# Seven block products of a gated feed-forward: lower left weights loaded twice, products reordered, operand sums in other buffers

## The chip, the cores and the metric

The kernel runs on one core of a Trainium2 chip. The metric is the device time of one execution in microseconds (us); less is better.

## What is computed

Two transformer blocks follow each other on 512 tokens of width 1024, all in float32. The first has a gated feed-forward network, a mixer (short convolution and attention), and a second gated feed-forward; the second block has its own mixer and feed-forward. The change touches the second feed-forward of the first block alone (`ffn2` in the inputs):

```python
def swiglu(x, w_gu, w_down):
    g, u = jnp.split(x @ w_gu, 2, axis=-1)
    return (jax.nn.silu(g) * u) @ w_down
...
        u = modulate(rmsnorm(h, norm3_g[l]), mod[:, 2, 0], mod[:, 2, 1])
        h = h + FFN_RES_WEIGHT * mod[:, 2, 2][:, None, :] * swiglu(u, ffn2_w_gu[l], ffn2_w_down[l])
```

The inner width is 2816, so `w_gu` is 1024 x 5632 and `w_down` 2816 x 1024.

## The kernel before

**How a float32 product is made.** Each operand is cut into a high part (`hi`, rounded by ScalarE on the copy) and a low part (`lo`, the rest, by VectorE); TensorE then adds three products, hi x hi, hi x lo and lo x hi. Line 131 makes `whi`, line 132 `wlo` of a weight tile; both kinds have four buffers. This is called a split below.

**How the stage is tiled.** The 2816 inner features are 22 blocks of 128, taken two at a time: 11 pairs. The first pair (`eight_pair`, line 652) multiplies in the plain way, lines 162 to 164. The other ten (`seven_pair`, line 670) take the gate block and the up block of the weights together as a 2 x 2 block matrix (rows: upper and lower half of the 1024 inputs; columns: gate and up), the activations as a 2 x 2 block matrix too (columns: upper and lower half of the tokens), and make the product with seven block products in place of eight, lines 536, 541 and 543. One block product is 24 matmuls of 256 columns, so a pair has 168.

**What the seven products need.** `load` (line 555) fetches the four weight blocks of a pair, each 128 x 1024 float32 (512 KB): w11 and w12 are the gate's upper and lower half of rows, w21 and w22 the up block's. w11 and w21 lie in tiles of the tag `ra` (four buffers), w12 and w22 together in one `raw` tile, of which there are two in the whole kernel; the weights of the down projection come through these two as well. `run` (line 571) needs four sums of weight blocks. They are made by DMAs that add into their target (line 578), issued by GpSimd; they work in place, so a sum that is written over a block has to wait until the split of that block has read it. On the other side the products need four sums of activation blocks, `usum` (lines 512 to 518), made once by VectorE in `operand` (line 508), split into `uth` and `utl`, and held for the whole stage. The tiles of `usum` take the four `ra` buffers too.

**The order in `run` before.** Products are named p1, p2, q7, q5, q6, q3, q4, in this order. p1, p2 and q3 multiply plain activations; q4 to q7 multiply sums of them.

```python
            p1 = split_w(w11)
            add(w11, w21)
            ...
            q7 = split_w(w11)
            add(w21, w22)
            add(w11, w22)
            ...
            q6 = split_w(w11)
            add(w11, w12)
            ...
            q3 = split_w(w11)
```

The results stand in four PSUM banks (`ca`, `cb`, `cc`, `cd`); ScalarE copies three of them out (line 582), VectorE combines them (lines 607 to 617), `upper` applies the gate function and `lower` multiplies and splits the result for the down projection.

**What sets the order of the work.** The framework orders the instructions of each engine when the kernel is built, by program order and by its own idea of when each can start; on the chip each engine then works through its list in that order, and an instruction that waits holds up all behind it on its engine. Loads are issued by SyncE's queue (SP), the adding DMAs by GpSimd's (POOL).

**Around it.** The pairs come in groups: pairs 2 to 4 of the stage, then a down projection of six features, again three pairs and six features, three and six, then one pair and the last four features (`bounds`, line 688). The down projection (lines 162 to 164 with `m_hi`, `m_lo`) is 128 x 512 matmuls.

Of the kernel before, what the change touches and what calls it, by code (L numbers as in the profile page):

```python
# [8 lines left out]
F32 = mybir.dt.float32  # L9
# [4 lines left out]
P = 128  # L14
D = 1024
# [10 lines left out]
def kernel(  # L26
# [7 lines left out]
    nc = tc.nc  # L34
# [13 lines left out]
    def z_bank(shape=(P, S)):  # L48
        return ps.tile(list(shape), F32, tag="z", name="z_ps")
# [32 lines left out]
    with tc.tile_pool(name="stage", bufs=1) as stage:  # L82
# [41 lines left out]
        def split_w(src, hi=None, lo=None):  # L124
            if hi is None:
                shape = [P, src.shape[1], src.shape[2]]
                hi, lo = (
                    wp.tile([P, 8 * P], F32R, tag=tag, name=tag, bufs=4)[
                        :, 0:shape[1] * shape[2]].rearrange("p (k n) -> p k n", n=shape[2])
                    for tag in ("whi", "wlo"))  # L130
            nc.scalar.activation(out=hi, in_=src, func=AF.Copy)  # L131
            nc.vector.tensor_tensor(out=lo, in0=src, in1=hi.bitcast(F32), op=ALU.subtract)  # L132
            return hi, lo
# [184 lines left out]
        class Modulated:  # L318
# [13 lines left out]
            def operand(self):  # L332
                u = new_u()
                for pb, cols in self.pieces:
                    modulate(self.sub, u, pb, cols)
                return u
# [163 lines left out]
    class Seven:  # L500
# [4 lines left out]
            self.pool = pool  # L505
            self.sums = []

        def operand(self, u, full):

            self.u = u  # L510
            for k in range(HK):
                t = self.pool.tile([P, 4, 256], F32, tag="ra", name="usum", bufs=4)
                b11, b12 = full[k][:, H1], full[k][:, H2]
                b21, b22 = full[k + HK][:, H1], full[k + HK][:, H2]
                nc.vector.tensor_sub(out=t[:, 0], in0=b11, in1=b12)
                nc.vector.tensor_sub(out=t[:, 2], in0=b12, in1=b22)
                nc.vector.tensor_sub(out=t[:, 1], in0=t[:, 2], in1=b11)
                nc.vector.tensor_add(out=t[:, 3], in0=t[:, 1], in1=b21)
                hi, lo = (self.pool.tile([P, 4, 256], F32R, tag=tag, name=tag, bufs=HK)
                          for tag in ("uth", "utl"))  # L520
                nc.scalar.activation(out=hi, in_=t, func=AF.Copy)
                nc.vector.tensor_tensor(out=lo, in0=t, in1=hi.bitcast(F32), op=ALU.subtract)
                self.sums.append((hi, lo))
# [31 lines left out]
        def load(self, a1, a2):  # L555
            def block(out, src):
                nc.sync.dma_start(out=out, in_=src.rearrange("(k p) n -> p k n", p=P))

            half = D // 2
            w11, w21 = (self.pool.tile([P, HK, 256], F32, tag="ra", name="w_sum", bufs=4)  # L560
                        for _ in range(2))
            raw = raw_tile()
            w12, w22 = (raw[:, i * 1024:(i + 1) * 1024].rearrange("p (k n) -> p k n", n=256)
                        for i in range(2))
            block(w11, a1[0:half])
            block(w21, a2[0:half])
            block(w12, a1[half:D])
            block(w22, a2[half:D])
            return w11, w12, w21, w22

        def run(self, weights, upper, lower):

            w11, w12, w21, w22 = weights

            def add(to, of):
                nc.gpsimd.dma_start(out=to, in_=of, accum_op=ALU.add)

            def copy(acc):  # L580
                v = self.ev()
                nc.scalar.activation(out=v, in_=acc, func=AF.Copy)
                return v

            p1 = split_w(w11)
            add(w11, w21)
            ca = z_bank()
            self.times(ca, p1, self.plain(0, H1), True)
            v1 = copy(ca)
            p2 = split_w(w12)  # L590
            self.times(ca, p2, self.plain(HK, H1), False)
            upper(ca, 0)
            q7 = split_w(w11)
            add(w21, w22)
            add(w11, w22)
            cd = z_bank()
            self.times(cd, q7, self.diff(2), True)
            v7 = copy(cd)
            q5 = split_w(w21)
            cc = z_bank()  # L600
            self.times(cc, q5, self.diff(0), True)
            v5 = copy(cc)
            q6 = split_w(w11)
            add(w11, w12)
            cb = z_bank()
            self.times(cb, q6, self.diff(1), True)
            nc.vector.tensor_add(out=v1, in0=v1, in1=cb)
            nc.vector.tensor_add(out=v5, in0=v5, in1=v1)
            nc.vector.tensor_sub(out=v7, in0=v7, in1=v5)
            q3 = split_w(w11)  # L610
            self.times(cc, q3, self.plain(HK, H2), False)
            nc.vector.tensor_add(out=v5, in0=cc, in1=v1)
            upper(v5, 1)
            lower(v7, 1)
            q4 = split_w(w22)
            self.times(cd, q4, self.diff(3), False)
            nc.vector.tensor_sub(out=v1, in0=cd, in1=v1)
            lower(v1, 0)

# [13 lines left out]
    def ffn_seven(nxt, w_gu, w_down, sub, on_final):  # L633
        with tc.tile_pool(name=f"ffn{sub}", bufs=4) as fp:
# [9 lines left out]
            def split_m(m, hi, lo):  # L644
                nc.scalar.activation(out=hi, in_=m, func=AF.Copy)
                nc.vector.tensor_tensor(out=lo, in0=m, in1=hi.bitcast(F32), op=ALU.subtract)

            def m_pair():
                return tuple(fp.tile([P, 2, S], F32R, tag=tag, name=name)
                             for tag, name in (("mh", "m_hi"), ("ml", "m_lo")))  # L650

            def eight_pair(f0):
                pair = m_pair()
                for r in range(2):
                    f = f0 + r
                    wg, wu = by_feature(load_pair(w_gu[:, f * P:(f + 1) * P],
                                                  w_gu[:, FF + f * P:FF + (f + 1) * P], KT, P))
                    for cols in (ALL,) if r else HALVES:
                        n = cols.stop - cols.start
                        pg = mm_bank()[:, 0:n]  # L660
                        proj(pg, wg, u, cols=cols)
                        pu = mm_bank()[:, 0:n]
                        proj(pu, wu, u, cols=cols)
                        sg = seven.ev()[:, 0:n]
                        nc.scalar.activation(out=sg, in_=pg, func=AF.Silu)
                        nc.vector.tensor_mul(out=sg, in0=sg, in1=pu)
                        split_m(sg, *(t[:, r, cols] for t in pair))
                return pair

            def seven_pair(f0):  # L670
# [15 lines left out]
                return pair  # L686

            bounds = ((0, 6), (6, 12), (12, 18), (18, 22))
            pairs = [eight_pair(0)]
            seven.operand(u, full)  # L690
            for f0, f1 in bounds:
                last = f1 == NF
                for f in range(f0 + 2, min(f1 + 2, NF), 2):
# [755 lines left out]
```

## Time and profile before

| what | value |
|---|---|
| three runs | 2166.06 us (median), 2164.12 to 2168.78 |
| the profiled execution | 2169.28 us |
| its span, first to last instruction | 2167.5 us |
| granted TensorE clock, mean of the span | 0.986 |
| TensorE (PE) busy | 2099.1 us, 97% |
| VectorE (DVE) busy | 1242.4 us, 57% |
| ScalarE (ACT) busy | 882.7 us, 41% |
| GpSimd (POOL) busy | 127.7 us, 6% |

PE is the matrix engine, PEld its weight load, which runs beside it. Times within the trace count from the first instruction. The seven-product stage lies between 810 us and 1171 us. In a timeline row the columns are start, duration, engine, line, operation, written tile, read tiles, shapes, number, and in brackets the idle time of that engine before the instruction and what ended it. A "q" behind an engine's name marks its queue. A row of busy time by stretch has the stretch, its length, then for PE, PEld, DVE, ACT and POOL the busy time and the number of instructions, then the granted clock, the share of time that the DMA engines were busy, and GB/s.

### The profile page before, as it was taken

The page shows a single profiled execution, that of the slowest core. Times are in us where ns is not written, and L with a number is a line of the kernel's source. Part 1 is how long each engine was busy: PE and PEld are TensorE (multiplying, and loading weights), DVE is VectorE, ACT ScalarE, POOL GpSimd, SP SyncE. Part 2 cuts the span into 40 slices and gives each one's busy share as a digit, 9 for nine tenths or more (in the row PEclk, how much of TensorE's full clock was granted, in tenths as well). Part 3 has the DMA queues.
Part 4 walks back from the last instruction along what each step waited for, and adds up shares of the span by engine and source line. Part 5 has one row for each costly group of instructions (what it writes and reads, how often), then busy time and mean ns, then how long its engine had stood idle before and what let it go on. Part 6 is the DMA issues. An engine that isn't in the chain of part 4 may idle for free.

```text
span 2167.5 us, 26690 instructions
## 1 busy us (share of the span) xinstructions
PE 2099.1 (97%) x10522; PEld 1737.5 (80%) x10522; DVE 1242.4 (57%) x2104; ACT 882.7 (41%) x1372; POOL 127.7 (6%) x196
## 2 busy tenths in 40 slices
PE   7999999999999997899989999998999999999998
PEld 5778888888878887888888877766888888888888
DVE  3775645557543474545456477754554566474665
ACT  4322222367643353333334454554233344242444
POOL 1000000000000001010100011111400000000000
PEclk9999999999999999999999999999999999999999
DMA  9766644331223336565544242221423333333332
GB/s 344 225 218 174 195 142 124 107 98 59 59 79 98 97 100 139 151 135 155 134 129 110 78 122 78 78 73 59 136 78 97 98 98 98 97 97 98 88 117 79
DMA packets 287569, 256.81 MB, mean 118 GB/s; under 512 B 7525, under 2 KB 269354, under 8 KB 287188
## 3 DMA queue, kind: packets, MB, share of 16 engines
q1 hardware_dynamic: 278336, 223.96, 33.9%
q0 software_dynamic: 8416, 30.06, 6.4%
q8 instruction: 83, 1.36, 0.3%
q10 hardware_dynamic: 692, 1.09, 0.1%
q14 instruction: 42, 0.34, 0.1%
HBM read 229.89 MB, written 4.23 MB: 108 GB/s over the span
## 4 chain that ended last, share of the span: by engine, by line
PE 47%; ACT 1%; issue 1%; DVE 1%; DMA 0%; POOL 0%; POOLq 0%; ACTq 0%; DVEq 0%
PE mm_ps L162 12%; PE mm_ps L164 12%; PE mm_ps L163 12%; PE mm_ps L174 2%; PE mm_ps L175 2%; PE mm_ps L176 2%; PE po_ps L1133 2%; PE z_ps L1126 1%; PE z_ps L1087 1%; PE z_ps L1089 1%; PE z_ps L543 0%; PE z_ps L541 0%; PE z_ps L536 0%; PE z_ps L1248 0%; DMA w_sum<-w_raw 0%
## 5 line engine op out<-in xcount | busy, mean ns | idle before, releaser
L131 ACT ACTIVATE whi<-w_raw 128x1024 fp32r<-128x1024 f32 (+2 forms) x338 | 344.4, 1023 | 704.7 <-PE mm_ps L163 550.4
L162 PE MATMUL mm_ps<-uh,whi 128*128 128x512 f32 (+1 forms) x1360 | 529.4, 391 | 5.1 <-ACT uh L307 2.0
L163 PE MATMUL mm_ps<-ul,whi 128*128 128x512 f32 x1360 | 529.5, 390 | 0.0
L164 PE MATMUL mm_ps<-uh,wlo 128*128 128x512 f32 x1360 | 528.4, 389 | 0.0
L132 DVE TENSOR_TENSOR wlo<-w_raw,whi 128x1024 fp32r<-128x1024 f32 (+2 forms) x338 | 402.3, 1193 | 149.7 <-ACT whi L131 145.6
L162 PEld LDWEIGHTS mm_ps<-uh,whi 128*128 128x128 f32 x1360 | 255.8, 189 | 60.7 <-ACT uh L307 3.9
L164 PEld LDWEIGHTS mm_ps<-uh,wlo 128*128 128x128 f32 x1360 | 256.0, 188 | 52.1 <-issue 1.6
L163 PEld LDWEIGHTS mm_ps<-ul,whi 128*128 128x128 f32 x1360 | 256.1, 188 | 51.8 <-issue 0.8
L162 PE MATMUL mm_ps<-m_hi,whi 128*128 128x512 f32 (+1 forms) x560 | 211.6, 381 | 0.9 <-ACT whi L131 0.5
L163 PE MATMUL mm_ps<-m_lo,whi 128*128 128x512 f32 (+1 forms) x560 | 211.3, 377 | 0.0
L164 PE MATMUL mm_ps<-m_hi,wlo 128*128 128x512 f32 (+1 forms) x560 | 211.1, 378 | 0.0
L162 PEld LDWEIGHTS mm_ps<-m_hi,whi 128*128 128x128 f32 x560 | 105.4, 188 | 21.1 <-ACT whi L131 0.9
L163 PEld LDWEIGHTS mm_ps<-m_lo,whi 128*128 128x128 f32 x560 | 105.5, 188 | 20.2 <-issue 0.4
L164 PEld LDWEIGHTS mm_ps<-m_hi,wlo 128*128 128x128 f32 x560 | 105.3, 188 | 20.0
L132 DVE TENSOR_TENSOR wlo<-w_sum,whi 128x1024 fp32r<-128x1024 f32 x50 | 61.2, 1225 | 103.8 <-ACT whi L131 103.0
L536 PE MATMUL z_ps<-uth,whi 128*128 128x256 f32 x320 | 94.6, 296 | 18.7 <-ACT whi L131 18.6
L174 PE MATMUL mm_ps<-whi,uh 128*128 128x512 f32 (+1 forms) x288 | 100.7, 353 | 5.9 <-ACT zv L1190 2.9
L131 ACT ACTIVATE whi<-w_sum 128x1024 fp32r<-128x1024 f32 x50 | 52.9, 1058 | 126.4 <-DMA w_sum<-w_raw 69.5
L175 PE MATMUL mm_ps<-wlo,uh 128*128 128x512 f32 (+1 forms) x288 | 99.0, 345 | 0.0
L176 PE MATMUL mm_ps<-whi,ul 128*128 128x512 f32 (+1 forms) x288 | 97.8, 345 | 0.0
L543 PE MATMUL z_ps<-uth,wlo 128*128 128x256 f32 x320 | 93.7, 293 | 3.6 <-DVE wlo L132 3.6
L541 PE MATMUL z_ps<-utl,whi 128*128 128x256 f32 x320 | 92.8, 290 | 0.0
(355 smaller groups left out, 3261.4 us busy)
## 6 DMA issues: line engine op xcount, KB each, us to landing
w_raw<-in_ffn_w_gu_dram SPq DMA_DIRECT2D x68, 512.0 KB, 5.2
ada_w<-in_w_ada_dram SPq DMA_DIRECT2D x28, 1024.0 KB, 5.2
w_raw<-in_w_up_dram SPq DMA_DIRECT2D x44, 512.0 KB, 5.2
w_raw<-in_w_in_dram SPq DMA_DIRECT2D x20, 1024.0 KB, 5.2
w_sum<-w_raw POOLq DMA_DIRECT2D x30, 512.0 KB, 4.6
w_raw<-in_ffn_w_down_dram SPq DMA_DIRECT2D x16, 768.0 KB, 4.4
w_raw<-in_w_mix_in_dram SPq DMA_DIRECT2D x24, 512.0 KB, 5.3
w_sum<-in_ffn_w_gu_dram SPq DMA_DIRECT2D x20, 512.0 KB, 3.6
```

The costliest lines, as they stand in the source:

```text
L131: nc.scalar.activation(out=hi, in_=src, func=AF.Copy)
L132: nc.vector.tensor_tensor(out=lo, in0=src, in1=hi.bitcast(F32), op=ALU.subtract)
L162: nc.tensor.matmul(acc, lhsT=a, rhs=uhi[:, cols], start=k == 0, stop=False)
L163: nc.tensor.matmul(acc, lhsT=a, rhs=ulo[:, cols], start=False, stop=False)
L164: nc.tensor.matmul(acc, lhsT=b, rhs=uhi[:, cols], start=False, stop=k == n - 1)
L174: nc.tensor.matmul(acc, lhsT=a, rhs=wh, start=k == 0, stop=False)
L175: nc.tensor.matmul(acc, lhsT=a, rhs=wl, start=False, stop=False)
L176: nc.tensor.matmul(acc, lhsT=b, rhs=wh, start=False, stop=k == kt - 1)
L536: i = nc.tensor.matmul(a, lhsT=whi[:, k, rows], rhs=uhi, start=start and first is None, stop=False, skip_group_check=True)
L541: nc.tensor.matmul(a, lhsT=whi[:, k, rows], rhs=ulo, start=False, stop=False, skip_group_check=True)
L543: nc.tensor.matmul(a, lhsT=wlo[:, k, rows], rhs=uhi, start=False, stop=last, skip_group_check=True)
L1133: nc.tensor.matmul(po[64 * hd:64 * hd + 64, b * P:S], lhsT=vts[head // 4][:, b, c0:c0 + 64], rhs=pT, start=b == 0, stop=b == NB - 1, skip_ ...
```

## The change

`load` fetches w21 a second time, into a third tile `s1`; the tag `ra` has five buffers in place of four. In `run`, `s1` becomes w21 + w22, then takes w11, then w12, one after the other; `w21` itself takes w11. So w11, w12 and w22 stay as loaded, and the first two sums, `add(s1, w22)` and `add(w21, w11)`, write over nothing that a split reads before. The order of products becomes q5, q7, p1, q6, p2, q4, q3. The loads come in the order s1, w22, w11, w21, w12. `usum` takes its tiles from the tag `ml` (which the low parts of the results use later), and its work moves from behind the first pair to the place between the two halves of it, before the buffers for that pair's result are taken.

```diff
-        def operand(self, u, full):
+        def operand(self, u, full, tag):
             self.u = u
+            self.raw = [self.pool.tile([P, 4, 256], F32, tag=tag, name="usum")
+                        for _ in range(HK)]
+            self.full = full
+
+        def steps(self):
             for k in range(HK):
-                t = self.pool.tile([P, 4, 256], F32, tag="ra", name="usum", bufs=4)
...
-            w11, w21 = (self.pool.tile([P, HK, 256], F32, tag="ra", name="w_sum", bufs=4)
-                        for _ in range(2))
+            w11, w21, s1 = (self.pool.tile([P, HK, 256], F32, tag="ra", name="w_sum", bufs=5)
+                            for _ in range(3))
...
+            block(s1, a2[0:half])
+            block(w22, a2[half:D])
             block(w11, a1[0:half])
             block(w21, a2[0:half])
             block(w12, a1[half:D])
-            block(w22, a2[half:D])
...
+            add(s1, w22)
+            add(w21, w11)
+            q5 = split_w(s1)
+            add(s1, w11)
+            cc = z_bank()
+            self.times(cc, q5, self.diff(0), True)
+            v5 = copy(cc)
+            q7 = split_w(w21)
+            cd = z_bank()
+            self.times(cd, q7, self.diff(2), True)
+            v7 = copy(cd)
             p1 = split_w(w11)
-            add(w11, w21)
             ca = z_bank()
             self.times(ca, p1, self.plain(0, H1), True)
             v1 = copy(ca)
+            q6 = split_w(s1)
+            add(s1, w12)
+            cb = z_bank()
+            self.times(cb, q6, self.diff(1), True)
+            nc.vector.tensor_add(out=v1, in0=v1, in1=cb)
             p2 = split_w(w12)
             self.times(ca, p2, self.plain(HK, H1), False)
             upper(ca, 0)
-            q7 = split_w(w11)
-            add(w21, w22)
-            add(w11, w22)
-            cd = z_bank()
-            self.times(cd, q7, self.diff(2), True)
-            v7 = copy(cd)
-            q5 = split_w(w21)
-            cc = z_bank()
-            self.times(cc, q5, self.diff(0), True)
-            v5 = copy(cc)
-            q6 = split_w(w11)
-            add(w11, w12)
-            cb = z_bank()
-            self.times(cb, q6, self.diff(1), True)
-            nc.vector.tensor_add(out=v1, in0=v1, in1=cb)
             nc.vector.tensor_add(out=v5, in0=v5, in1=v1)
             nc.vector.tensor_sub(out=v7, in0=v7, in1=v5)
-            q3 = split_w(w11)
+            q4 = split_w(w22)
+            self.times(cd, q4, self.diff(3), False)
+            q3 = split_w(s1)
             self.times(cc, q3, self.plain(HK, H2), False)
             nc.vector.tensor_add(out=v5, in0=cc, in1=v1)
             upper(v5, 1)
             lower(v7, 1)
-            q4 = split_w(w22)
-            self.times(cd, q4, self.diff(3), False)
             nc.vector.tensor_sub(out=v1, in0=cd, in1=v1)
             lower(v1, 0)
...
             def eight_pair(f0):
-                pair = m_pair()
+                made = []
...
+                        made.append((sg, r, cols))
+                    if r == 0:
+                        seven.steps()
+                        pair = m_pair()
+                    for sg, r, cols in made:
                         split_m(sg, *(t[:, r, cols] for t in pair))
+                    made = []
...
+            seven.operand(u, full, "ml")
             pairs = [eight_pair(0)]
-            seven.operand(u, full)
```

## Rows read from the trace of the kernel before

**Rows 1.** The page: span, share and count of TensorE; its granted clock by slice.

```profile
PE 2099.1 (97%) x10522; PEld 1737.5 (80%) x10522; DVE 1242.4 (57%) x2104; ACT 882.7 (41%) x1372; POOL 127.7 (6%) x196
...
PEclk9999999999999999999999999999999999999999
```

**Rows 2.** Busy time by stretch: the four groups of seven-product pairs.

```profile
810.00:899.00 89.00, 72.42 (x512) 69.16 (x511) 41.54 (x49) 31.86 (x42) 10.59 (x12) 0.90 0.64 153
930.00:1008.00 78.00, 69.37 (x511) 67.42 (x511) 38.74 (x44) 30.95 (x40) 7.83 (x9) 0.91 0.63 151
1040.00:1118.00 78.00, 68.20 (x508) 65.87 (x508) 38.73 (x44) 30.73 (x40) 7.84 (x9) 0.93 0.58 138
1150.00:1171.00 21.00, 21.00 (x174) 20.82 (x173) 10.70 (x14) 8.72 (x13) 0.87 (x1) 1.00 0.41 98
```

**Rows 3.** The same view: the first pair, and a down projection.

```profile
782.00:810.00 28.00, 25.33 (x152) 21.79 (x153) 25.36 (x58) 22.93 (x44) 0.70 (x1) 1.00 0.28 87
...
1118.00:1150.00 32.00, 32.00 (x145) 26.52 (x144) 16.64 (x20) 8.73 (x11) 2.61 (x3) 1.00 0.43 109
```

**Rows 4.** Timeline of TensorE, two matmuls of a block product without a wait.

```profile
951.14 0.28 PE L541 MATMUL z_ps<-ul,whi 128*128 128x256 f32 x1
951.26 0.28 PE L543 MATMUL z_ps<-uh,wlo 128*128 128x256 f32 x1
```

**Rows 5.** Groups by line from 810 to 1171 us: TensorE's idle time, last columns.

```profile
L536 PE MATMUL z_ps<-uth,whi 128*128 128x256 f32 x320 | 94.6, 296 | 18.7 <-ACT whi L131 18.6
...
L543 PE MATMUL z_ps<-uth,wlo 128*128 128x256 f32 x320 | 93.7, 293 | 3.6 <-DVE wlo L132 3.6
L536 PE MATMUL z_ps<-uh,whi 128*128 128x256 f32 x240 | 74.1, 309 | 12.2 <-ACT whi L131 10.5 <-ACT ev L582 1.7
```

**Rows 6.** Timeline of ScalarE: the splits of the second seven-product pair, and the next.

```profile
832.32 1.04 ACT L131 ACTIVATE whi<-w_sum 128x1024 fp32r<-128x1024 f32 x1
...
845.00 1.06 ACT L131 ACTIVATE whi<-w_sum 128x1024 fp32r<-128x1024 f32 x1 [2.22 <-DMA w_sum<-w_sum]
...
852.54 1.06 ACT L131 ACTIVATE whi<-w_sum 128x1024 fp32r<-128x1024 f32 x1 [0.69 <-DMA w_sum<-w_raw]
...
860.25 1.06 ACT L131 ACTIVATE whi<-w_sum 128x1024 fp32r<-128x1024 f32 x1 [2.90 <-DMA w_sum<-w_raw]
...
862.16 1.04 ACT L131 ACTIVATE whi<-w_sum 128x1024 fp32r<-128x1024 f32 x1
```

**Rows 7.** Timeline of VectorE: the low part of one split.

```profile
846.08 1.22 DVE L132 TENSOR_TENSOR wlo<-w_sum,whi 128x1024 fp32r<-128x1024 f32 x1 [2.58 <-ACT whi L131]
```

**Rows 8.** Timeline of GpSimd: two sums of the same pair, issue only.

```profile
835.29 0.87 POOL L578 DMA_DIRECT2D w_sum<-w_sum  x1 [8.62 <-DVE wlo L132]
845.17 0.87 POOL L578 DMA_DIRECT2D w_sum<-w_raw  x1 [9.01 <-DMA w_sum<-w_sum]
```

**Rows 9.** Waits from 810 to 1171 us: us in total, times, longest.

```profile
POOL w_sum L578 <- DVE wlo L132: 244.8, 28, 36.8
```

**Rows 10.** DMA issues from 800 to 1171 us, last column median us to landing.

```profile
w_sum<-w_raw POOLq DMA_DIRECT2D x30, 512.0 KB, 4.6
w_sum<-in_ffn_w_gu_dram SPq DMA_DIRECT2D x20, 512.0 KB, 3.6
...
w_raw<-in_ffn_w_gu_dram SPq DMA_DIRECT2D x16, 512.0 KB, 5.2
w_sum<-w_sum POOLq DMA_DIRECT2D x10, 512.0 KB, 6.7
```

**Rows 11.** The sums of line 578 alone: from issue to landing.

```profile
DMA to landing us min/median/max: 4.5/4.7/9.6
```

**Rows 12.** Timelines of SyncE's queue and VectorE: first block loads, last activation sum.

```profile
804.16 28.95 SPq L557 DMA_DIRECT2D w_sum<-in_ffn_w_gu_dram  x6
...
806.94 1.22 DVE L522 TENSOR_TENSOR utl<-usum,uth 128x1024 fp32r<-128x1024 f32 x1
```

**Rows 13.** Timeline of TensorE: the first matmul of the seven-product stage.

```profile
810.18 0.28 PE L536 MATMUL z_ps<-uh,whi 128*128 128x256 f32 x1
```

More of the change, by code (lines that the diff above doesn't have):

```diff
@@ L506, in __init__ @@
             self.sums = []
-        def operand(self, u, full):
+        def operand(self, u, full, tag):
             self.u = u
+            self.raw = [self.pool.tile([P, 4, 256], F32, tag=tag, name="usum")
+                        for _ in range(HK)]
+            self.full = full
+        def steps(self):
             for k in range(HK):
-                t = self.pool.tile([P, 4, 256], F32, tag="ra", name="usum", bufs=4)
-                b11, b12 = full[k][:, H1], full[k][:, H2]
-                b21, b22 = full[k + HK][:, H1], full[k + HK][:, H2]
+                t = self.raw[k]
+                b11, b12 = self.full[k][:, H1], self.full[k][:, H2]
+                b21, b22 = self.full[k + HK][:, H1], self.full[k + HK][:, H2]
                 nc.vector.tensor_sub(out=t[:, 0], in0=b11, in1=b12)
@@ L567, in load @@
             block(w12, a1[half:D])
-            block(w22, a2[half:D])
-            return w11, w12, w21, w22
+            return w11, w12, w21, w22, s1
         def run(self, weights, upper, lower):
-            w11, w12, w21, w22 = weights
+            w11, w12, w21, w22, s1 = weights
             def add(to, of):
```

## Prediction

> **What bounds the kernel now.** I began with the page. TensorE is busy for 97% of the span, and its clock stands at 9 tenths or more in every slice [rows 1], so nothing seems left to gain; but an average over forty slices hides a stage. The view of busy time by stretch shows it. In the groups of three seven-product pairs TensorE is busy for 72.4 of 89 us, 69.4 of 78 and 68.2 of 78, and the granted clock is 0.90 to 0.93 [rows 2]; in the down projection between them it is busy throughout at clock 1.00 [rows 3]. So the stage loses time in idle gaps, and then again because stretches behind such gaps run at the lower of the two clock levels (1.2 in place of 2.4 GHz).
>
> How much is lost? Matmuls of a block product that wait for nothing start 0.12 us apart [rows 4]. Ten pairs of 168 make 1680, which is 201.6 us. The four stretches last 89 + 78 + 78 + 21 = 266 us and hold 512 + 511 + 508 + 174 = 1705 matmuls [rows 2]; the other 25 belong to the down projection, at 32.0 / 145 = 0.22 us each [rows 3], 5.5 us. 266 - 201.6 - 5.5 = **58.9 us are lost**. Of these 18.7 + 3.6 + 12.2 = 34.5 us are idle time, nearly all of it ended by a split [rows 5]; the remaining 24 us are the lower clock and the pipeline starting again.
>
> What are the splits waiting for? The timeline of ScalarE for the second pair reads as one chain [rows 6]: the split of w11 at 832.32, then those of the three sums written over it at 845.00, 852.54 and 860.25, and at 862.16 w11 of the next pair. That is a **loop** of 12.7 + 7.5 + 7.7 + 1.9 = 29.8 us. One link is a split (1.06 us high part, the low part ends at 847.30 [rows 7], so 2.3 us), then a sum that may start only now because it overwrites what the split read, then the next split, which waits for it. GpSimd's queue says the same from its side: 244.8 us of waiting for the low part [rows 9]. A link costs 2.6 us beside the sum's own landing time: 7.6 us less about 5. The landing time is 4.7 us in the median, up to 9.6 [rows 11]; the late ones are the first sums of a pair (median 6.7 against 4.6 [rows 10]), and the sum issued at 835.29 held up the next one, which GpSimd could issue only at 845.17 [rows 8]. TensorE needs 168 x 0.12 = 20.2 us for a pair and waits for a loop of nearly 30. Only the pair behind a down projection escapes: the fourth group, one such pair, shows 21.00 of 21 us busy [rows 2].
>
> **The change, part by part.**
>
> *Two sums freed of a split.* s1 + w22 and w21 + w11 now need loads alone, and can be made while the pair before is multiplied. In series remain: split q5, sum, split q6, sum, split q3, then q5 of the next pair on ScalarE. That is two links where there were three: 2 x 7.6 + 1.1 to 1.9 = 16 to 17 us, under the 20.2 us of TensorE. With both sums at the slow median the loop is 2 x (2.6 + 6.7) + 1.4 = 20.0 us, still just under; with both at 9.6 it is 25.8 us, 5.6 over. I take 0.9 us of waiting a pair, near the undisturbed rows since most sums land in 4.6: for nine pairs 8 us, with bounds of 0 and 9 x 5.6 = 50 us.
>
> *Reordering.* Between the start of q5 and that of q6 lie three products, 8.6 us, over a link of 7.6; between q6 and q3 three again. So each sum is covered by products that don't need it. If that cover were shorter by one product (2.9 us) each link would show by about 2 us. Number and size of splits, copies and combinations are the same, so VectorE stays at about half of a stretch [rows 2]: 0 us.
>
> *The second load of w21.* Ten DMAs more of 512 KB, landing in 3.6 us (block loads) to 5.2 us (those of the raw tile) [rows 10]. SP's queue has room for them, and the DMA engines are at 0.58 to 0.64 of their time [rows 2]. They cost nothing by themselves, because a pair's loads are due a pair ahead; what they cost is slower sums beside them, which is in the bounds above.
>
> *Buffers.* Three `ra` tiles a pair out of five: two are free for the next pair at once, the third when the first sum or split of this pair has released one, a link, 7.6 us, into it at the latest. A late third load delays the early sums only, by 3.6 to 5.2 us out of more than 10 of slack: 0.
>
> *Activation sums in other buffers, and earlier.* Before, `usum` held the `ra` buffers and the first block load was issued at 804.16; now it can go earlier. In return the first product needs the activation sums, which p1 and p2 did not. The last low part of them ends at 806.94 + 1.22 = 808.2, and TensorE begins the stage at 810.18 [rows 12, 13], so there are 2 us of cover in a stretch where VectorE is busy for 25.4 of 28 us [rows 3]. Moving this work ahead of the second half's results does not add to it. If q5's and q7's low parts come first, at 1.22 each [rows 7], the cover is gone and 0.5 us shows. I take 1 us, bounds -1 to 3.
>
> *The end.* q3 now comes last and passes through the gate function before it is multiplied: one more ScalarE step at the end of the last pair, at most 1.1 us by the split, which is twice as wide [rows 6]. I take 1 us, bounds 0 and 2.
>
> **Sum.** 58.9 - 8 - 1 - 1 = 48.9 us. The profiled execution took 2169.28 us (span 2167.5), which would become 2120.4; the median of the runs is 3.2 us lower, so the forecast is 2166.06 - 48.9 = 2117, put at **2118 us**. With all bounds at their best it is 2166 - 60 = 2106.
>
> **Rivals.**
>
> *The sums get slower.* The same DMA engines carry five block loads a pair in place of four, and they bunch where buffers come free, which is while a sum of the pair is under way. For it: first sums beside loads already take 6.7 in the median and up to 9.6 [rows 10, 11]. Against it: the sum in the loop is no longer the one behind the loads of a new pair. With both sums at 8.9 us the loop is 24.4 us, 4.2 over TensorE, 9 x 4.2 = 38 us lost: 58.9 - 38 - 2 = 19 us gained, 2147 us. The Trainium skill ("DMA: Bandwidth & Descriptors", section "Queues, rings and completion order") says that each DMA engine goes round-robin between the queues that have work for it, so a load on SP's queue takes turns with a sum on GpSimd's; by that rule the added load speaks against the change. The rows of slow first sums agree with it.
>
> *The early sums aren't early.* Each engine's list is fixed ahead. If s1 + w22 of the next pair stands behind a waiting sum or split, three links stay in series and the time stays within 0.2% of 2166. Against it: that sum waits for no instruction of this pair, and the last sum of the pair before is issued with three products, 8.6 us, still to be multiplied.
>
> *Slower: the loads wait for buffers.* If the block for s1 gets the buffer that q3's split frees at the end of a pair, the loop becomes load, sum, split q5, sum, split q6, sum, split q3. Its price is 3.6 + 0.3 + 4.7 + 2 x 7.6 + 2.3 = 26 us with quick transfers, and 5.2 + 0.3 + 9.6 + 2 x 12.2 + 2.3 = 42 with late landings, where the pairs now take 26.6 in the mean; nearer the quick end, I put 30: 9 x 30 + 20 = 290 in place of 266, 2190 us. It decides from 27.2 us a pair on. For it: two of the five buffers must serve three loads. Against it: s1 is the first load of a pair, and two buffers are free from the pair before.
>
> **How the numbers follow.** My forecast (TensorE bound, 2106 to 2130) gets 0.68, slower sums 0.17, no early sums 0.06, loads waiting 0.09. Both of the first two are faster: 0.85; same 0.06; slower 0.09. About 0.2%, 4.3 us, is what a measurement of this kernel tells from no change. From 2106 the range reaches over the forecast and most of the slower-sums case, to 2150.
>
> **What would show it.** Right: in the three-pair stretches TensorE busy above 95% and its clock near 1.00, pairs about 20 to 21 us apart, the first two sums of a pair issued before the last split of the pair before, GpSimd's waits for the low part halved in number. Slower sums: landing medians of 7 us or more, with splits of q6 or q3 ending TensorE's idle time. Loads waiting: the s1 load issued behind q3's split. Wrong altogether if pairs still lie 26 us apart or TensorE's idle time in the stage stays above 25 us.

## The result, and the profile after

The changed kernel takes **2117.97 us** (median of four runs, 2113.32 to 2118.2) against 2167.42 for the kernel before (four runs, 2164.12 to 2170.28): a ratio of **0.9767 [0.9747, 0.9788]**. The forecast was 2118. Three of the four runs took 2117.74 to 2118.2 us at a mean granted clock of 0.992, the fourth 2113.32 at 0.996, so differences of 4 or 5 us from this kernel say little by themselves. The profiled execution took 2118.2 us, with a span of 2116.5 (before 2167.5): 51.0 us less.

The view of busy time by stretch, for the stage and for the 24 us ahead of it (columns as in [rows 2]); the down projections between the groups are left out as before:

```profile
782.00:806.00 24.00, 20.97 (x128) 19.19 (x128) 21.44 (x54) 20.07 (x41) 3.51 (x4) 0.86 0.82 220
806.00:878.00 72.00, 67.85 (x526) 66.31 (x526) 46.05 (x53) 35.10 (x47) 8.72 (x10) 0.98 0.75 180
911.00:972.00 61.00, 61.00 (x508) 60.91 (x507) 38.68 (x44) 30.55 (x40) 7.80 (x9) 1.00 0.79 198
1004.00:1066.00 62.00, 62.00 (x511) 61.54 (x511) 39.38 (x45) 31.25 (x41) 7.78 (x9) 1.00 0.74 182
1098.00:1123.00 25.00, 25.00 (x190) 23.91 (x189) 13.87 (x18) 10.21 (x15) 0.86 (x1) 1.00 0.31 85
```

Read it against [rows 2], with the prediction's own working. The four stretches are 72 + 61 + 62 + 25 = 220 us in place of 266. They hold 526 + 508 + 511 + 190 = 1735 matmuls, 55 of them foreign to the stage, 55 x 0.22 = 12.1 us. 220 - 201.6 - 12.1 = **6.3 us are lost, where 58.9 were**: 52.6 us recovered. Both parts of the loss went together: the second and third groups have no idle time, and their granted clock is 1.00 where it was 0.91 and 0.93. Only the first group still loses something.

The groups by line from 806 to 1123 us show what is left of TensorE's idle time (last columns):

```profile
L541 PE MATMUL z_ps<-uth,whi 128*128 128x256 f32 x320 | 90.6, 283 | 0.3 <-ACT whi L131 0.3
...
L548 PE MATMUL z_ps<-uth,wlo 128*128 128x256 f32 x320 | 90.5, 283 | 0.0
L541 PE MATMUL z_ps<-uh,whi 128*128 128x256 f32 x240 | 69.0, 288 | 3.8 <-ACT ev L588 3.8
```

In [rows 5] these three had 34.5 us, nearly all ended by a split; now it is 4.1 us, and 3.8 of it is ended by a **copy** of a result (line 588), as 1.7 us were in [rows 5]. The timeline of ScalarE in the second seven-product pair shows where that comes from:

```profile
824.89 1.06 ACT L131 ACTIVATE whi<-w_sum 128x1024 fp32r<-128x1024 f32 x1 [4.16 <-DMA w_sum<-w_raw]
...
826.33 1.05 ACT L131 ACTIVATE whi<-w_sum 128x1024 fp32r<-128x1024 f32 x1
...
838.63 1.06 ACT L131 ACTIVATE whi<-w_sum 128x1024 fp32r<-128x1024 f32 x1 [6.36 <-DMA w_sum<-w_sum]
...
847.61 1.06 ACT L131 ACTIVATE whi<-w_sum 128x1024 fp32r<-128x1024 f32 x1 [3.36 <-DMA w_sum<-w_raw]
848.57 0.58 ACT L588 ACTIVATE ev<-z_ps 128x512 f32<-128x512 f32 x1
```

These are q3's split of the pair before, then q5's, q6's and q3's of this one, and the copy of p1's result. From q3 to q3 it is 22.7 us, where [rows 6] had 29.8. The copy stands behind q3's split in ScalarE's list, the split waits 3.36 us for its sum, and TensorE, whose next product goes into the bank that the copy reads, waits too. In the timeline of TensorE:

```profile
826.48 0.38 PE L541 MATMUL z_ps<-uh,whi 128*128 128x256 f32 x1 [1.51 <-ACT ev L588]
...
849.20 0.58 PE L541 MATMUL z_ps<-uh,whi 128*128 128x256 f32 x1 [2.31 <-ACT ev L588]
```

GpSimd's timeline over the same pair shows the two early sums of the next pair (829.42 and 840.39) going out well before this pair's last split at 847.61. Right behind each stands one of this pair's own two sums (829.96 and 841.24):

```profile
829.42 0.86 POOL L584 DMA_DIRECT2D w_sum<-w_raw  x1 [10.65 <-DMA w_raw<-in_ffn_w_gu_dram]
829.96 1.21 POOL L584 DMA_DIRECT2D w_sum<-w_sum  x1
840.39 0.86 POOL L584 DMA_DIRECT2D w_sum<-w_sum  x1 [9.22 <-DMA w_sum<-in_ffn_w_gu_dram]
841.24 0.90 POOL L584 DMA_DIRECT2D w_sum<-w_raw  x1
```

The waits from 806 to 1123 us say the same in total (us, times, longest). What was 28 waits for the low part [rows 9] is 10; most of GpSimd's waiting is for loads now:

```profile
POOL w_sum L584 <- DMA w_raw<-in_ffn_w_gu_dram: 104.5, 7, 30.6
POOL w_sum L584 <- DMA w_sum<-in_ffn_w_gu_dram: 68.4, 9, 9.2
POOL w_sum L584 <- DVE wlo L132: 65.0, 10, 11.4
```

### The profile page after: what moved, and what is told of

The parts are those of the page before. It is cut to its first block, busy times and chain, and to the rows that moved or that the text cites. A ratio compares the mean times of both kernels' runs of the same rounds, so it can differ in the third digit from the quotient of the medians.

```text
span 2116.5 us, 26729 instructions
## 1 busy us (share of the span) xinstructions
PE 2078.4 (98%) x10522; PEld 1723.9 (81%) x10522; DVE 1243.4 (59%) x2104; ACT 882.0 (42%) x1372; POOL 126.9 (6%) x196
## 4 chain that ended last, share of the span: by engine, by line
PE 93%; DMA 2%; DVE 2%; ACT 1%; issue 1%; SPq 1%; POOL 0%; POOLq 0%; ACTq 0%; DVEq 0%
PE mm_ps L162 23%; PE mm_ps L164 23%; PE mm_ps L163 23%; PE z_ps L541 3%; PE z_ps L546 3%; PE z_ps L548 3%; PE mm_ps L174 2%; PE mm_ps L175 2%; PE mm_ps L176 2%; PE po_ps L1145 2%; PE z_ps L821 1%; PE z_ps L1138 1%; PE z_ps L1099 1%; DMA w_sum<-in_ffn_w_gu_dram 1%; DMA w_sum<-w_raw 1%
## 5 line engine op out<-in xcount | busy, mean ns | idle before, releaser
L164 PEld LDWEIGHTS mm_ps<-m_hi,wlo 128*128 128x128 f32 x560 | 105.3, 188 | 20.2
```

The lines of the kernel that those rows point to most:

```text
L164: nc.tensor.matmul(acc, lhsT=b, rhs=uhi[:, cols], start=False, stop=k == n - 1)
```

## The experiments

Each run is compared with the kernel before on the same chip (medians 2168.1 to 2169.6 there). Medians in us, ratios to the kernel before with 95% intervals. A hundredth of a per cent is 0.22 us.

| run | what it is | median | ratio |
|---|---|---|---|
| changed kernel | | 2117.97 | 0.9767 [0.9747, 0.9788] |
| buffers_only | kernel before, with the buffers and the early activation sums | 2165.32 | 0.9974 [0.9963, 0.9985] |
| old_order | changed, products in the old order | 2169.52 | 0.9997 [0.9988, 1.0007] |
| q5_split_first | old_order, q5's split at the head of the pair | 2151.38 | 0.9926 [0.991, 0.9943] |
| double_load | changed, one more load a pair | 2125.64 | 0.9795 [0.9778, 0.9813] |
| ra4 | changed, four `ra` buffers | 2145.13 | 0.9881 [0.9865, 0.9897] |
| ra3 | changed, three `ra` buffers | 2138.24 | 0.986 [0.9846, 0.9875] |
| ra4_sum_order | ra4, early sums behind the last sum of the pair before | 2113.47 | 0.9747 [0.9733, 0.9762] |
| usum_ra | changed, activation sums back in `ra` | 2123.91 | 0.9792 [0.9779, 0.9806] |
| pow_first | changed, sums behind a small GpSimd operation | 2114.31 | 0.9749 [0.9736, 0.9762] |
| copy_first | changed, q3's split behind the copy | 2111.64 | 0.9735 [0.9722, 0.9748] |
| both_first | the last two together | 2110.37 | 0.9729 [0.9716, 0.9742] |
| ra4_all_orders | ra4_sum_order and both_first together | 2110.52 | 0.9729 [0.9716, 0.9743] |

### Which part brings the gain

**buffers_only.** The kernel before with five `ra` buffers, `usum` in `ml` and made between the halves of the first pair; loads, sums and order of products as before.

```diff
-            w11, w21 = (self.pool.tile([P, HK, 256], F32, tag="ra", name="w_sum", bufs=4)
+            w11, w21 = (self.pool.tile([P, HK, 256], F32, tag="ra", name="w_sum", bufs=5)
...
+            seven.operand(u, full, "ml")
             pairs = [eight_pair(0)]
-            seven.operand(u, full)
```

> The kernel before with the buffers of the change alone: five ra buffers, activation sums in the ml tiles and made between the halves of the first pair; weights loaded once, sums and order of products as before. Theory (a loop of three splits and three sums in series binds a pair): nothing of the loop changes, so 2161 to 2168 us, TensorE idle in the stage still about 30 to 35 us. Rival (the gain is from buffers, loads that can go earlier): 2125 to 2145 us.

Measured 0.9974: a gain of about 5.6 us, small but clear of no change. TensorE's idle time for splits is nearly that of [rows 5] (18.6, 1.9 and 13.7 us in the same three groups). So nine tenths of the gain come only with the rest of the change.

**old_order.** The changed kernel with loads, early sums and buffers as they are, but the products in the order p1, p2, q7, q5, q6, q3, q4 (the diff shows the splits and sums as they stand then).

```diff
             add(s1, w22)
             add(w21, w11)
+            p1 = split_w(w11)
...
+            p2 = split_w(w12)
...
+            q7 = split_w(w21)
...
             q5 = split_w(s1)
             add(s1, w11)
...
             q6 = split_w(s1)
             add(s1, w12)
...
             q3 = split_w(s1)
...
+            q4 = split_w(w22)
```

> The changed kernel with its two early sums, but the products in the order of before (p1, p2, q7, q5, q6, q3, q4). Theory: the loop has two sums in series as in the changed kernel, but the sum behind q6 is now covered by one product (2.9 us) and not by three, over a link of 7.6 us, so 3 to 5 us of waiting in each of the seven or nine pairs not covered by a down projection: 2140 to 2160 us. Rival (only the number of sums in series counts): 2116 to 2124 us.

A miss: **no gain at all**, 0.9997. The sums are free of the splits and early, yet TensorE waits as long as before; even the little that buffers_only gained is not to be seen. Groups by line from 806 to 1175 us, then ScalarE's timeline:

```profile
L541 PE MATMUL z_ps<-uth,whi 128*128 128x256 f32 x320 | 93.1, 291 | 4.8 <-ACT whi L131 4.7
...
L548 PE MATMUL z_ps<-uth,wlo 128*128 128x256 f32 x320 | 91.0, 284 | 2.6 <-DVE wlo L132 2.5
...
L541 PE MATMUL z_ps<-uh,whi 128*128 128x256 f32 x239 | 75.4, 316 | 29.5 <-ACT whi L131 29.5
```

```profile
829.51 1.06 ACT L131 ACTIVATE whi<-w_sum 128x1024 fp32r<-128x1024 f32 x1 [4.71 <-DMA w_sum<-w_raw]
...
835.89 1.06 ACT L131 ACTIVATE whi<-w_sum 128x1024 fp32r<-128x1024 f32 x1 [2.48 <-PE z_ps L546]
838.82 1.06 ACT L131 ACTIVATE whi<-w_sum 128x1024 fp32r<-128x1024 f32 x1 [1.34 <-issue]
...
850.01 1.06 ACT L131 ACTIVATE whi<-w_sum 128x1024 fp32r<-128x1024 f32 x1 [7.88 <-DMA w_sum<-w_sum]
...
858.49 1.06 ACT L131 ACTIVATE whi<-w_sum 128x1024 fp32r<-128x1024 f32 x1 [5.96 <-DMA w_sum<-w_raw]
```

These are q3 of the pair before, q7, q5, q6, q3. The loop is 9.3 + 11.2 + 8.5 = 29.0 us, as long as in [rows 6]. Its first part, from q3 to q5, is where the freed sums should have paid: q5's data had long been there (its sum went out at 799.08), but its split is the fourth of its pair in ScalarE's list, and the splits in front of it wait until TensorE has let go of a buffer of `whi` (2.48 us "<-PE z_ps" for q7). A link was taken out of the data, and the list put another in its place. The two links behind q5 then have one product each to cover them.

**q5_split_first.** To part the two: old_order, with q5's split and the sum behind it moved to the head of the pair, the product left fourth.

```diff
             add(s1, w22)
             add(w21, w11)
+            q5 = split_w(s1)
+            add(s1, w11)
             p1 = split_w(w11)
...
-            q5 = split_w(s1)
-            add(s1, w11)
```

> The kernel of the old product order with its two early sums, in which only the split for q5 and the sum behind it are moved to the head of the pair; TensorE's order of products stays p1, p2, q7, q5, q6, q3, q4. In the old order the split for q5 began 9.3 us behind that for q3, as the fourth in ScalarE's list with four buffers for split weights, so the loop was 9.3 + 11.2 + 8.5 = 29 us in spite of two sums in series. Theory (the loop counts, and in it the place of q5's split): the split follows that for q3 at once, the loop falls to 17 to 22 us, 2118 to 2138 us. Rival (the order of the products themselves counts, since the sum behind q6 has one product as cover): 2150 us or more.

It stays where the rival had it: 0.7 of the 2.3 per cent are recovered, some 15 us, and that is what the list position of one split and its sum is worth. What remains is 19.4 us of idle time ended by copies. In the same window:

```profile
L541 PE MATMUL z_ps<-uth,whi 128*128 128x256 f32 x320 | 94.2, 296 | 19.4 <-ACT ev L588 19.4
```

ScalarE's timeline: q3's split of the pair before, then q6's and q3's of this pair, the last one waiting, and two copies behind it:

```profile
825.29 1.06 ACT L131 ACTIVATE whi<-w_sum 128x1024 fp32r<-128x1024 f32 x1 [10.09 <-PE z_ps L548]
...
839.19 1.06 ACT L131 ACTIVATE whi<-w_sum 128x1024 fp32r<-128x1024 f32 x1 [0.64 <-PE z_ps L546]
...
850.20 1.06 ACT L131 ACTIVATE whi<-w_sum 128x1024 fp32r<-128x1024 f32 x1 [4.10 <-DMA w_sum<-w_raw]
...
853.05 1.06 ACT L588 ACTIVATE ev<-z_ps 128x512 f32<-128x512 f32 x2
```

The loop is 24.9 us here, and not the 17 to 22 expected: q6's split comes 13.9 us behind q3's, and q3's 11.0 behind that. So the new order pays by starting the loop early in the pair. That it pays a second time, by putting products between the links, fits what remains, but no run parts this from the two copies behind q3's split.

### What loads and buffers cost

**double_load.** The block for `s1` is fetched twice; its second copy is not needed.

```diff
             block(s1, a2[0:half])
+            block(s1, a2[0:half])
```

> The changed kernel with the block for s1 fetched twice in a row into the same tile, so that each pair moves another 512 KB and the early sum starts one landing (3.6 to 5.2 us) later. Theory (loads cost nothing by themselves, a pair's loads are early): 2116 to 2124 us. Rival (loads beside the sums slow them, and the added load of the change already costs): 2130 us or more, with landing medians of the sums at 6.5 us or more.

Between the two: the median is 6 us above the changed kernel's when taken by ratio (0.0028), with intervals that overlap. The trace goes the same way: TensorE's idle time behind copies is 8.4 us (3.8 after), and the medians from issue to landing of the two kinds of sum are 6.0 and 5.2 us (5.1 and 5.0 after). If ten more loads cost anything, it is little; a cost clear of the noise is not shown.

**ra4 and ra3.** Four and three `ra` buffers in place of five.

```diff
-            w11, w21, s1 = (self.pool.tile([P, HK, 256], F32, tag="ra", name="w_sum", bufs=5)
+            w11, w21, s1 = (self.pool.tile([P, HK, 256], F32, tag="ra", name="w_sum", bufs=4)
```

> The changed kernel with four ra buffers as before, so one buffer and not two is free for the next pair's three loads. Theory: s1 takes the free one, w11 and w21 wait for the first splits and sums of the pair before, some 8 us into it, and still land a dozen us early: 2116 to 2128 us. Rival (the loads wait for buffers): the early sums move to the end of the pair, a third link in series, 2150 to 2190 us.

> The changed kernel with three ra buffers, so that no load of the next pair can begin before this pair has freed a tile, and the one for s1 or w11 only with the split for q3. Theory (my rival of loads that wait for buffers, priced at 30 us a pair): load, sum, split, sum, split, sum, split in series, 2180 to 2230 us. Rival (the down projections and three early products cover it): 2140 to 2165 us.

Both missed. Four buffers lose 25 us of the gain (0.0114) and land between theory and rival; three lose no more than four, and come out far under what was expected. So it isn't a shortage that grows with each buffer taken away. GpSimd's timeline of ra4 shows what it is:

```profile
830.27 0.86 POOL L584 DMA_DIRECT2D w_sum<-w_raw  x1 [2.90 <-DMA w_sum<-in_ffn_w_gu_dram]
841.06 0.86 POOL L584 DMA_DIRECT2D w_sum<-w_sum  x1 [9.93 <-DMA w_sum<-in_ffn_w_gu_dram]
841.60 1.21 POOL L584 DMA_DIRECT2D w_sum<-w_raw  x1
```

The row at 841.06 is an early sum of the next pair, waiting 9.93 us for its load. The row at 841.60 is the last sum of this pair, next in the list. It could have gone out some 7 us earlier: q6's split began at 832.12 in this run, and the low part is done 2.3 us later. ScalarE's timeline shows who pays:

```profile
848.28 1.06 ACT L131 ACTIVATE whi<-w_sum 128x1024 fp32r<-128x1024 f32 x1 [9.42 <-DMA w_sum<-w_raw]
849.24 0.58 ACT L588 ACTIVATE ev<-z_ps 128x512 f32<-128x512 f32 x1
```

q3's split waits, the copy behind it waits, and TensorE idles 20.3 us in the stage behind copies in plain products (line 541, `uh`). With five buffers the same order stands in the list (840.39 ahead of 841.24 above), but there q6's low part is itself done only at about 838.63 + 2.3 = 840.9, so the wait in front of the last sum costs next to nothing (0.3 us).

**ra4_sum_order.** If that is the cause, four buffers suffice as soon as the early sums stand behind the last sum of the pair before. (`tc.issue_after(x)` keeps an instruction behind `x` in the framework's order.)

```diff
-            w11, w21, s1 = (self.pool.tile([P, HK, 256], F32, tag="ra", name="w_sum", bufs=5)
+            w11, w21, s1 = (self.pool.tile([P, HK, 256], F32, tag="ra", name="w_sum", bufs=4)
...
-                nc.gpsimd.dma_start(out=to, in_=of, accum_op=ALU.add)
+                self.added = nc.gpsimd.dma_start(out=to, in_=of, accum_op=ALU.add)
...
+            with tc.issue_after(self.added.ins) if self.added else nullcontext():
-            add(s1, w22)
-            add(w21, w11)
+                add(s1, w22)
+                add(w21, w11)
```

> The kernel with four ra buffers, and the two early sums of a pair kept behind the last sum of the pair before in GpSimd's list. With four buffers the early sum of the next pair stood ahead of the last sum of this pair and waited up to 9.9 us for its load. Theory (the buffers cost time by way of that list): the last sum goes out on time, 2116 to 2128 us. Rival (the loads themselves are too late, wherever the sums stand): 2138 us or more.

0.9747, 29 us better than ra4, a little below the 2116 to 2128 us expected, and no slower than the changed kernel with its five. GpSimd's list now has the last sum and the next pair's first (one row, x2) released by the low part, and the load's wait behind them:

```profile
840.16 1.75 POOL L585 DMA_DIRECT2D w_sum<-w_raw  x2 [10.84 <-DVE wlo L132]
841.47 1.32 POOL L585 DMA_DIRECT2D w_sum<-w_sum  x1
```

Three buffers with the list order unchanged do no worse than four. In ra3's second pair the wait for a load stands at another place, as GpSimd's timeline and then ScalarE's show:

```profile
831.89 0.86 POOL L584 DMA_DIRECT2D w_sum<-w_sum  x1 [1.57 <-DMA w_sum<-in_ffn_w_gu_dram]
844.21 1.75 POOL L584 DMA_DIRECT2D w_sum<-w_raw  x2 [11.45 <-DMA w_sum<-in_ffn_w_gu_dram]
```

```profile
837.84 2.95 ACT L131 ACTIVATE whi<-w_sum 128x1024 fp32r<-128x1024 f32 x3 [8.08 <-DMA w_sum<-w_sum]
```

The sum at 831.89 is w21 + w11 of this pair itself, no longer early, and the splits of q7, p1 and q6 wait for it until 837.84. q6's low part is then done by 843.0, so the last sum (one of the two at 844.21) loses about 1 us behind the early one, where it lost 7 in ra4. TensorE's idle time behind splits and copies in the stage is 17.3 us, in ra4 23.9. That this is all of the difference is not shown.

**usum_ra.** The activation sums back in the tag `ra`, still made early.

```diff
-            self.raw = [self.pool.tile([P, 4, 256], F32, tag=tag, name="usum")
+            self.raw = [self.pool.tile([P, 4, 256], F32, tag=tag, name="usum", bufs=5)
...
-            seven.operand(u, full, "ml")
+            seven.operand(u, full, "ra")
```

> The changed kernel with the activation sums back in the ra buffers, now five. Theory: the w11, w21 loads of the first seven-product pair wait for the activation sums, so its early sums come some 10 us later; the first pair then waits for them by up to 10 us, once: 2120 to 2130 us. Rival (other buffers for the activation sums do nothing): 2116 to 2119 us.

As expected, 0.9792, though its interval overlaps the changed kernel's. The trace has the mechanism: the first block loads wait for `ra`, q7's split is late, and TensorE stands still at the start of the stage. Its timeline:

```profile
820.08 0.58 PE L541 MATMUL z_ps<-uth,whi 128*128 128x256 f32 x1 [4.57 <-ACT whi L131]
```

Together with buffers_only this makes it likely, and no more, that about 5 us of the gain belong to the other buffers.

### What is left, and a faster version

**copy_first.** q3's split is put behind the copy of p1's result in ScalarE's list.

```diff
-                nc.scalar.activation(out=v, in_=acc, func=AF.Copy)
+                self.copied = nc.scalar.activation(out=v, in_=acc, func=AF.Copy)
...
+            copied = self.copied
...
-            q3 = split_w(s1)
+            with tc.issue_after(copied.ins):
+                q3 = split_w(s1)
```

> The changed kernel with the split for q3 kept behind the copy of the p1 result on ScalarE. In the changed kernel TensorE's two longest waits in the stage, 1.51 and 2.31 us, end on that copy, which stood in ScalarE's list behind the split that waits for the last sum. Theory: with the copy ahead both waits go, and 1.3 us of lower clock behind the second: 4 to 5 us less than the changed kernel, about 2113 us. Rival (product p2 would only wait for something else, or the list changes elsewhere): within 1.5 us of the changed kernel.

It went the theory's way: 0.9735, some 7 us under the changed kernel in the median (4 to 5 were expected), with intervals that overlap by 0.0001. The group that idled 3.8 us is clean (groups by line of this kernel, 806 to 1123 us):

```profile
L541 PE MATMUL z_ps<-uth,whi 128*128 128x256 f32 x320 | 90.7, 284 | 0.4 <-ACT whi L131 0.3
...
L541 PE MATMUL z_ps<-uh,whi 128*128 128x256 f32 x240 | 68.0, 283 | 0.0
```

**pow_first.** Ahead of the stage, the changed kernel issues its first early sum on GpSimd after a wait of 6.47 us; the small operation of line 260 stands behind it, and TensorE waits 1.55 us for that. The changed kernel's timelines of GpSimd and TensorE:

```profile
785.91 0.99 POOL L584 DMA_DIRECT2D w_sum<-w_raw  x1 [6.47 <-ACT u_full L634]
786.61 1.05 POOL L260 TENSOR_TENSOR inv<-var,mhalf 128x2 f32<-128x2 f32 x1
```

```profile
787.71 1.23 PE L266 MATMUL z_ps<-ident,inv 128*128 128x128 f32 x4 [1.55 <-POOL inv L260]
```

In pow_first the sums come behind that operation.

```diff
-                nc.gpsimd.dma_start(out=to, in_=of, accum_op=ALU.add)
+                with tc.issue_after(last_pow[0].ins):
+                    nc.gpsimd.dma_start(out=to, in_=of, accum_op=ALU.add)
```

> The changed kernel with the sums kept behind the small power on GpSimd that the normalization ahead of the stage needs. In the changed kernel the first early sum stood ahead of it on GpSimd and waited for its load, TensorE then sat idle 1.55 us in place of 0.19 us before the broadcast (line 266), and the clock was at its lower level for 6.8 us from 784 us on. Theory: this is a wait that the change added, worth 1.4 us of idle time and about 2.6 us of lower clock: 3 to 4 us less than the changed kernel, about 2114 us. Rival (the lower clock there has another cause): 0 to 1.5 us less.

The median is where it was expected, but the interval overlaps the changed kernel's, and the trace says why the edit can't have brought much: the 1.55 us wait is gone, and 7 us later another of 1.61 us, which the kernel before had and the changed kernel had not, is back (pow_first's timeline of TensorE):

```profile
794.88 0.39 PE L162 MATMUL mm_ps<-uh,whi 128*128 128x256 f32 x1 [1.61 <-ACT ev L672]
```

Inconclusive: idle time moved rather than went, and the changed kernel's own fourth run is as fast.

**both_first and ra4_all_orders.** copy_first and pow_first together; then the same with ra4_sum_order's order and four buffers (its early sums of the first pair stand behind line 260's operation, the others behind the last sum). The diff is of the second.

```diff
+            with tc.issue_after((self.added or last_pow[0]).ins):
+                add(s1, w22)
+                add(w21, w11)
...
+            with tc.issue_after(copied.ins):
+                q3 = split_w(s1)
```

> Both of the edits above, power first and copy first, in one kernel. Theory: they lie in different stretches and add up, 7 to 9 us less than the changed kernel, about 2110 us. Rival: one of the waits moves and returns elsewhere, 0 to 4 us less.

> Four ra buffers and all three orders together: early sums behind the last sum of the pair before on GpSimd, the first of them behind the small power, the split for q3 behind the copy of p1's result on ScalarE. Theory: what is left of waiting in the stage is head-of-list waiting, so this comes to 2108 to 2112 us, like the kernel with power and copy first and five buffers (2110 us). Rival (the fifth buffer is worth something once the copies are out of the way): 2114 us or more.

Both came as expected: 0.9729, with intervals wholly below the changed kernel's. They are the fastest versions in the median, some 8 us (0.0038) under it, and the second needs one buffer fewer; their intervals do not part them from copy_first or ra4_sum_order.

## Why the prediction was right, and where its steps were not

**What bounds the kernel, and the loss of 58.9 us: right.** The time came out of exactly the stretches where it was seen to be lost, the lower clock went with the idle time, and TensorE is the bound of the stage now. The 24 us that were put down to the clock and to restarts fit the granted clock of [rows 2]: 0.10 x 89 + 0.09 x 78 + 0.07 x 78 = 21.4 us. buffers_only, which leaves the loop, keeps the idle time; the changed kernel, which shortens it, has none in two groups of three pairs.

**Two sums freed, residual 8 us: right in size.** 6.3 us are lost in all, 0.7 a pair. The forecast loop of 16 to 20 us hides behind TensorE's 20.2; the one pair followed above, whose loop stayed visible, took 22.7, and the pair behind it 20.5.

**"They cost nothing by themselves ... slower sums beside them": about right.** The landing times of all sums became (line 584, to be read against [rows 11])

```profile
DMA to landing us min/median/max: 4.5/5.2/10.4
```

half a microsecond more in the median, far from the 8.9 of that rival. But this median mixes early sums with those in the loop. In the pair followed above the two sums in the loop (829.96 and 841.24) let their splits start 8.7 and 6.4 us after their issue (838.63 and 847.61): there the sums were slow as in that rival, and what the new order puts in front of q6 and q3 covered all but the 2.31 us at 849.20. The round-robin rule of the Trainium skill ("DMA: Bandwidth & Descriptors", section "Queues, rings and completion order"), by which a load on one queue takes turns with a sum on another, agrees in direction with double_load, where the landing medians rose to 6.0 and 5.2 us from 5.1 and 5.0; the 6 us in time that go with it are not clear of the noise.

**"Reordering ...: 0 us" failed as a reading of the parts.** It was right that the new order covers each link. But the prediction put the whole gain on the freed sums and only about 2 us a link on cover. The freed sums in the old order bring nothing (old_order), and the reorder is worth all of the 50 us (0.0230) on top of them; what it would bring without them was not tried. What was missed is that a split is bound by its place in ScalarE's list and by the four `whi` buffers as much as by its data; q5_split_first sizes the place in the list at some 15 us; how the other 35 divide between the cover and the copies behind q3's split stays open.

**"Buffers ... 0": right for five, for a reason that is thin.** The step asked when loads land and gave the early sums 10 us of slack. It didn't ask what stands behind an early sum on GpSimd while it waits. With five buffers the pair's own sums do, but the early ones have gone out by the time these are ready, and some 0.3 us is lost; with four the last sum waits 7 us in the pair followed, and 25 us go (ra4), all of which come back by order alone (ra4_sum_order).

**Activation sums, "I take 1 us" of cost: not borne out.** Made early and elsewhere, together with the fifth buffer, they gain about 5 us (buffers_only), outside the bounds of -1 to 3; usum_ra, which moves the sums alone back, points the same way, with an interval that overlaps. Start and end together cannot have cost more than a little: 52.6 us were recovered in the stage and 51.0 in the span. Of the gap of 1.6 us, 0.7 is there already at 778 us, ahead of the first early sum (line 260's operation before that starts at 778.71, and at 777.99 before). The rest may lie in the stretch from 782 to 806 us, with its wait on GpSimd's small operation, which the prediction had not seen: it costed GpSimd's sums and not what would stand behind the first of them.

**Rivals.** The early sums were early (829.42 and 840.39 before 847.61). old_order has that rival's time by another way: sums that are early, and splits that are not. The slower case didn't occur, and its price of 30 us a pair stays untested: even with three buffers s1 was not the block that came late (q5's split follows q3's of the pair before at once, 825.84 behind 824.39), and that kernel took 2138 us.

**What was to show it.** TensorE was to be busy for over 95%: it is 67.85 of 72 us, 94%, in the first group and all of the other two. Pairs were to lie 20 to 21 us apart: 22.7 and 20.5 in the first group. GpSimd's waits for the low part were to halve, and fell from 28 to 10.

So the time was right because the sum rested on what TensorE must do at least, which the runs bear out, and not on how the gain was dealt out among the parts, where the steps above failed. That would have shown had the parts not come together: the freed sums alone were worth nothing. That it was right to a tenth of a microsecond is luck: the kernel's own runs are 4.9 us apart, and the residual, start and end were each estimates that only happen to add up.

## What to carry to other kernels

When a dependency is taken out of a loop, ask what stands ahead of the freed instruction in its engine's list and which buffers it needs: the gain comes only if the order lets it start. When work is prefetched on a queue that goes in order, ask what is due now behind the prefetch; putting it behind the last urgent instruction made four buffers as good as five here. And a small instruction behind a waiting large one (a copy of 0.58 us behind a split) can hold the bound engine for the large one's wait.

## What the runs showed that was not expected

Fewer buffers were not steadily worse: 0.9881 with four, 0.986 with three (intervals that just overlap).

A sum that goes out right behind another lands late. The one issued at 829.96, half a microsecond behind an early sum, let its split start at 838.63, 8.7 us later, where a sum takes 4.5 us at the least; and in the whole kernel the longest took 10.4 us. Block loads were under way beside it too, and how much each adds was not parted.

The granted clock from 782 to 806 us was 0.86 in the changed kernel, where [rows 3] have 1.00 for 782 to 810, though TensorE's waits in it are no longer: 1.29 + 0.39 + 1.55 = 3.2 us against 1.29 + 0.39 + 0.19 + 1.61 = 3.5 before. With pow_first's edit, which moves a wait, the stretch has 0.93. What sets it there stays open.
